# Seven-product units in parts 0 and 1 of both down projections, with tiles of their own for single blocks

## The chip, the cores and the metric

The kernel runs on one core of one Trainium2 chip. The metric is the device time of one execution in microseconds (us). Before the change the median of three runs is 2259.6 us (2258.87 to 2261.23).

## The reference, cut to what matters

A decoder of two layers on 256 tokens of width 2048: a gated linear attention layer, then a forgetting-attention layer, each followed by a channel mixer. All is fp32. The change touches only the channel mixer, whose hidden width is 5632:

```python
def conv_ffn(h, w_up, conv_w, conv_b, w_down):
    u = causal_dwconv(h @ w_up, conv_w, conv_b)
    a, val = split_cols(u, [FFN_HIDDEN, FFN_HIDDEN])
    return (jax.nn.silu(a) * val) @ w_down
...
        h = rmsnorm(x, norm_ffn[i])
        x = x + conv_ffn(h, ffn_w_up[i], conv_w[i], conv_b[i], ffn_w_down[i])
```

## The kernel before, in words

**Products.** Each fp32 matrix product is made of three float32r products: activations (the stationary side, 128x128) and weights (the moving side, 128x512) are each split into a high and a low half, and high·high, low·high and high·low are summed in PSUM. The activations lie in `A` or `B` tiles, 16 of them, one for each 128 features, with both halves.

**Weights.** They stream from HBM in units of 128x1024 (two 128-row blocks of 512 columns): a DMA on SyncE's queue into `raw` (4 buffers), a ScalarE copy to the high half `whi` (3 buffers; L207 for plain units, L308 in seven-product units) and a VectorE subtraction to the low half `wlo` (3 buffers; L216 and L310). TensorE uses a plain unit in 12 matmuls of 512 columns: 2 token blocks x 2 row blocks x 3.

**The channel mixer.** `ffn` runs three parts (`PARTS`: hidden blocks 0-16, 16-32, 32-44). Each part has the up projections of its blocks (8, 8 and 6 panels; `proj_tm`, lines L228, L229, L232) and then the down projection of those blocks onto the four 512-column panels of `x` (`add_out`). What an up panel leaves goes by VectorE transposes and a DRAM turn to feature order, then through `taken` (convolution L995 to L997, SiLU L999, product L1000, split to halves L463, L464); these steps are due 8 and 9 weight units after the panel, so those of a part's last panels run during its down projection.

**Seven-product units.** A plain pair of units (two 512-column panels, two row blocks) is a 2x2 by 2x2 block product over token blocks, row blocks and panels: 8 products, 24 matmuls. `proj_seven` does chosen units with seven products, 21 matmuls, by the Strassen-Winograd scheme. The sums of activations are made in `summed` (tiles `forms`). The sums of weights `t13` and `t24` are made on VectorE from two raw units (L333 to L336). Four pairs of halves are made: v0 (raw, 1024 wide), v1 (one raw block, 512 wide, in a full 1024-wide buffer), v2 (`t13`) and v3 (`t24`). Four of the products go to PSUM tiles of their own (m1 `ps_t`, m5 and m7 `ps_s`, m6 `ps_o`); after the last such unit `more` adds them into `x` with eight operations (L951 to L958). The four `acc` tiles, all that PSUM holds of them, are added into `x` by `evac` (L939) at the end of the call; the next call's first matmul needs the first of them free.

**Where they are used before.** `SEVEN` names the units of each part: 3 and 5, 3 and 5, 2 and 4. Layer 0 uses them in all four panels of parts 0 and 1 (two calls of `proj_seven` each) and in the first two panels of part 2, ten pairs in all. Layer 1 gets no `forms` tiles, since it holds the pool `store` (final gain `gf`, output `y`, and extra `whi`/`wlo` buffers `spare` for the last panel) from its start, so it has none: its first two panels run in `proj_two`, the others in `proj_tm`.

**What sets the order.** The code gives priorities (a unit's load and split are moved ahead by 300 places, a seven-product unit's sums by 340), and a scheduler writes each engine's instructions into one fixed order from them. Each engine then works its own list in order; an instruction that waits holds what is behind it.

Of the kernel before, what the change touches and what calls it, by code (L numbers as in the profile page):

```python
# [36 lines left out]
NVER = 96  # L37
NUNIT = 1024
AHEAD = 300
SEVEN = ((3, 5), (3, 5), (2, 4))  # L40

SPREAD = [128 * q + 32 * k + i for k in range(4) for i in range(32) for q in range(4)]

# [93 lines left out]
def _trunk(ctx: ExitStack, tc: tile.TileContext, xt, xtok, memt, wp, wgu, gns, gfin, cnv, par, msk, out):  # L137
# [131 lines left out]
    def proj_seven(keys, src, forms, evacs, pool, more):  # L269
# [33 lines left out]
        def token(kc, b):  # L303
            return [src[kc - base][:, i, b * P : (b + 1) * P] for i in range(2)]

        def halves(raw, w, name="w"):
            hi = wpool.tile([P, NUNIT], F32R, name="whi", tag="whi", bufs=3)
            casts.append(S.activation(hi[:, :w], raw, AF.Copy))  # L308
            lo = wpool.tile([P, NUNIT], F32R, name="wlo", tag="wlo", bufs=3)
            V.tensor_tensor(lo[:, :w], raw, hi[:, :w].bitcast(F32), ALU.subtract)  # L310
            return hi, lo

        def load(unit):
# [5 lines left out]
        for u in range(count):  # L319
            k0, k1 = units[0][u][1]  # L320
            if u not in forms:
                for i in range(2):
                    hi, lo = split_unit(units[i][u])
                    emit([form(acc[i][b], token(kc, b), hi, lo, c) for b in range(2) for c, kc in enumerate((k0, k1))])
                    if u == count - 1:
                        for b in range(2):
                            evacs[i](b, acc[i][b])
                continue
            s = forms[u]
            with tc.high_priority(offset=AHEAD + 40):  # L330
                r0, r1 = (load(units[i][u]) for i in range(2))
                t13, t24 = (pool.tile([P, 2, 512], F32, name=n, tag=n) for n in ("t13", "t24"))
                V.tensor_tensor(t13[:, 0, :], r1[:, :512], r0[:, :512], ALU.subtract)  # L333
# [12 lines left out]
            with tc.high_priority(offset=AHEAD):  # L346
                v3 = halves(t24.rearrange("p c n -> p (c n)"), NUNIT)
            passed()
            emit([form(m6, s(1), *v3, 0), form(acc[0][1], token(k1, 1), *v3, 1)])
            if u == max(forms):  # L350
                more(m1, m5, m6, m7, pool)

    def turned(pool, bank, width, col):

# [578 lines left out]
            add_out(("wo", 1), mix, then, late=2)  # L933


    def add_out(key, src, then=None, spare=None, late=1, forms=None, pool=None):
        def evac(f):
            def out(b, a):
                V.tensor_tensor(x[f][:, b, :], x[f][:, b, :], a, ALU.add)  # L939
                if then is not None:  # L940
                    then(f, b)

            return out

        def seven(f):
            x0, x1 = x[f], x[f + 1]

            def more(m1, m5, m6, m7, pool):
                u = pool.tile([P, 512], F32, name="u", tag="us", bufs=2)
                w = pool.tile([P, 512], F32, name="w", tag="us", bufs=2)  # L950
                V.tensor_tensor(x0[:, 0, :], x0[:, 0, :], m1, ALU.add)  # L951
                S.activation(u, m1, AF.Copy)
                V.tensor_tensor(u, u, m6, ALU.add)
# [3 lines left out]
                V.tensor_tensor(x1[:, 1, :], x1[:, 1, :], w, ALU.add)  # L957
                V.tensor_tensor(x1, x1, m5.unsqueeze(1).to_broadcast([P, 2, 512]), ALU.add)  # L958

            proj_seven([(*key, g) for g in (f, f + 1)], src, forms, [evac(f), evac(f + 1)], pool, more)  # L960

        if forms:
            seven(0)
        else:
            proj_two([(*key, f) for f in range(2)], src, [evac(f) for f in range(2)], late)
        if forms and then is None:
            seven(2)
            return
        for f in range(2, 4):
            proj_tm((*key, f), src, evac(f), spare if f == 3 else None)  # L970

    def ffn(l, nx, h, m, then, spare=None):
        with tc.tile_pool(name=f"ffn{l}", bufs=1) as fp:
# [12 lines left out]

            def taken(j, base, u, i):
# [14 lines left out]
                if (j - base) // 2 in forms[base]:  # L1002
                    held.append(cv[1])
                    if i:
                        summed(forms[base][(j - base) // 2])

            def summed(form):
                h0, h1 = (natural(h) for h in held)
                held.clear()
                f = fp.tile([P, 4, P], F32, name="sf", tag="sf")  # L1010
# [7 lines left out]
            def panel(j, base, slack=0):  # L1018
# [14 lines left out]

                return evac

            for p, (lo, hi) in enumerate(PARTS):
# [6 lines left out]
                end = p == len(PARTS) - 1  # L1043
                add_out(("down", l, p), m, then if end else None, spare if end else None,
                        forms={u: form(t) for u, t in forms[lo].items()}, pool=fp)

    def preparing(name, dst):
        n = StreamNorm()
# [28 lines left out]


    fin = StreamNorm()
    with tc.tile_pool(name="store", bufs=1) as op:  # L1080
# [29 lines left out]
        ffn(1, n, bufA, bufB, then, op)  # L1110


def _constants():
# [82 lines left out]
```

## Time and profile before

| what | value |
| --- | --- |
| median of three runs | 2259.6 us |
| the profiled execution | 2260.52 us |
| its span, first to last instruction | 2258.7 us |
| mean granted TensorE clock | 0.999 |
| layer 0, down projection of part 0 (L290) | 645.1 to 732.1 us |
| the same of part 1 | 906.3 to 993.4 us |
| layer 0, part 2, first two panels (L290) | 1124.1 to 1159.9 us |
| layer 1, down projection of part 0 (plain) | 1704.9 to 1791.9 us |
| the same of part 1 | 1966.0 to 2053.1 us |

The profile is of one execution. All times in it are in us from its first instruction. In a timeline a row has start, duration, engine, source line, operation, output and inputs with shape, a count if the row merges several instructions of one kind that follow each other, and in brackets how long the engine had been idle before and what ended it. "PE" is TensorE's matmul, "DVE" VectorE, "ACT" ScalarE, "SPq" a DMA issued by SyncE. A matmul's duration (about 0.39 us here) is longer than the distance from one to the next, since they overlap; in a row that merges n of them, the distance is (duration - 0.39) / (n - 1).

### The profile page before, as it was taken

Reading aid. Unit: us, or ns where it says so; the run is one execution under the profiler, and the core shown is the slowest. Engines: PE = TensorE matmul, PEld = TensorE weight load, DVE = VectorE, ACT = ScalarE, POOL = GpSimd, SP = SyncE. Lnnn points to the kernel's source line nnn. Section 1 sums busy time; section 2 is a strip of 40 time slices with the busy share of each in tenths; the row PEclk is TensorE's granted clock in tenths of the full one; section 3 lists DMA queues with packets and bytes.
Section 4 is the critical chain, followed back from the end, with each engine's and each line's share of the span. In section 5 each row is a group of like instructions: output and inputs, shape, how many; then the busy total and the mean of one; then the engine's idle time right before and its main releaser. Section 6 shows DMA issues by size and latency. Waiting matters only on the chain.

```text
span 2258.7 us, 29424 instructions
## 1 busy us (share of the span) xinstructions
PE 2238.1 (99%) x10306; PEld 1866.9 (83%) x10306; DVE 1595.0 (71%) x2442; ACT 1298.8 (58%) x1881; POOL 2.9 (0%) x15
## 2 busy tenths in 40 slices
PE   9999999999999999999999999999999999999998
PEld 7888887888878888788878998888888888888886
DVE  7568987667778677876786656766776467754766
ACT  7555666556664566545665655555665355544654
POOL 0000000000000000000000000000000000000000
PEclk9999999999999999999999999999999999999999
DMA  8876666677876778658778886677877677766784
GB/s 318 279 234 190 207 202 215 194 244 243 252 214 205 236 239 242 207 200 247 238 234 249 259 270 202 179 246 235 251 242 226 195 236 243 242 202 209 239 244 149
DMA packets 303772, 516.97 MB, mean 229 GB/s; under 512 B 178556, under 2 KB 187272, under 8 KB 303496
## 3 DMA queue, kind: packets, MB, share of 16 engines
q1 hardware_dynamic: 124296, 427.24, 59.1%
q10 hardware_dynamic: 179328, 87.85, 13.8%
q8 instruction: 81, 1.33, 0.2%
q14 instruction: 67, 0.55, 0.1%
HBM read 470.44 MB, written 44.58 MB: 228 GB/s over the span
## 4 chain that ended last, share of the span: by engine, by line
PE 94%; DMA 2%; DVE 2%; ACT 1%; issue 1%; ACTq 0%; SPq 0%; DVEq 0%
PE acc L228 28%; PE acc L229 28%; PE acc L232 28%; PE acc L290 7%; DMA xturned<-square 1%; PE ps_s L290 1%; DVE wlo L216 0%; PE ps_s L768 0%; DMA raw<-wp 0%; DMA cb<-cdram 0%; PE ps_s L570 0%; PE ps_t L563 0%; ACT whi L207 0%; PE ps_o L581 0%; DMA back<-turned 0%
## 5 line engine op out<-in xcount | busy, mean ns | idle before, releaser
L216 DVE TENSOR_TENSOR wlo<-raw,whi 128x1024 fp32r<-128x1024 f32 (+4 forms) x789 | 942.9, 1199 | 550.0 <-ACT whi L207 520.6
L207 ACT ACTIVATE whi<-raw 128x1024 fp32r<-128x1024 f32 (+4 forms) x789 | 820.6, 1042 | 792.7 <-PE acc L229 575.5
L228 PE MATMUL acc<-whi,B 128*128 128x512 f32 (+3 forms) x1792 | 686.1, 384 | 1.0 <-ACT whi L207 0.8
L229 PE MATMUL acc<-whi,B 128*128 128x512 f32 (+3 forms) x1792 | 684.5, 383 | 0.0
L232 PE MATMUL acc<-wlo,B 128*128 128x512 f32 (+3 forms) x1792 | 470.0, 382 | 0.0
L228 PE MATMUL acc<-whi,A 128*128 128x512 f32 x1136 | 443.7, 392 | 1.5 <-ACT A L463 1.0
L229 PE MATMUL acc<-whi,A 128*128 128x512 f32 x1136 | 441.4, 390 | 0.0
L228 PEld LDWEIGHTS acc<-whi,B 128*128 128x128 f32 x1792 | 336.3, 188 | 62.8 <-ACT whi L207 1.6
L229 PEld LDWEIGHTS acc<-whi,B 128*128 128x128 f32 x1792 | 336.0, 188 | 59.5
L232 PEld LDWEIGHTS acc<-wlo,B 128*128 128x128 f32 x1792 | 333.5, 188 | 59.8
L232 PE MATMUL acc<-wlo,A 128*128 128x512 f32 x1136 | 305.6, 390 | 0.2 <-DVE wlo L216 0.2
L228 PEld LDWEIGHTS acc<-whi,A 128*128 128x128 f32 x1136 | 213.1, 188 | 48.3 <-ACT whi L207 2.0
L232 PEld LDWEIGHTS acc<-wlo,A 128*128 128x128 f32 x1136 | 213.0, 188 | 44.7 <-DVE wlo L216 0.7
L229 PEld LDWEIGHTS acc<-whi,A 128*128 128x128 f32 x1136 | 213.3, 188 | 44.2 <-DVE A L467 0.4
L290 PE MATMUL acc<-whi,A 128*128 128x512 f32 x488 | 127.5, 391 | 3.4 <-DVE A L464 1.4
L995 ACT ACTIVATE cv<-u,cw 128x256 f32<-128x256 f32 x176 | 97.2, 589 | 25.8 <-DMA u<-turned 25.6
L290 PEld LDWEIGHTS acc<-whi,A 128*128 128x128 f32 x488 | 91.1, 188 | 25.1 <-DVE A L464 1.8
L996 DVE SCALAR_TENSOR_TENSOR cv<-u,cw,cv 128x256 f32<-128x256 f32 x176 | 78.4, 478 | 18.0 <-ACT cv L995 18.0
L383 DVE STREAM_TRANSPOSE square<-scaled 128x512 f32<-128x512 f32 x122 | 79.9, 690 | 0.0
L997 DVE SCALAR_TENSOR_TENSOR cv<-u,cw,cv 128x256 f32<-128x256 f32 x176 | 77.2, 476 | 0.0
L290 PE MATMUL acc<-wlo,A 128*128 128x512 f32 x244 | 68.3, 390 | 0.0
L1025 ACT ACTIVATE scaled<-acc,ny 128x512 f32<-128x512 f32 x88 | 54.9, 674 | 0.0
(221 smaller groups left out, 1234.8 us busy)
## 6 DMA issues: line engine op xcount, KB each, us to landing
raw<-wp SPq DMA_DIRECT2D x743, 512.0 KB, 4.2
turned<-square ACTq DMA_DIRECT2D x61, 512.0 KB, 4.2
u<-turned ACTq DMA_DIRECT2D x176, 128.0 KB, 5.1
raw<-wp SPq DMA_DIRECT2D x32, 384.0 KB, 3.5
raw<-wp SPq DMA_DIRECT2D x24, 388.0 KB, 4.5
back<-xturned ACTq DMA_DIRECT2D x64, 128.0 KB, 5.2
xturned<-square ACTq DMA_DIRECT2D x12, 512.0 KB, 4.8
back<-turned ACTq DMA_DIRECT2D x32, 128.0 KB, 4.4
```

Of the source, the lines that this page charges most:

```text
L207: casts.append(S.activation(hi[:, s], raw[:, s], AF.Copy))
L216: V.tensor_tensor(lo[:, s], raw[:, s], hi[:, s].bitcast(F32), ALU.subtract)
L228: TE.matmul(acc[:, :n], xh, hi[:, s], start=first and j == 0, stop=False)
L229: TE.matmul(acc[:, :n], xl, hi[:, s], start=False, stop=False)
L232: TE.matmul(a, xh, ls, start=False, stop=stop)
L290: TE.matmul(a, x, w, start=k not in begun, stop=calls[k] == 0)
L383: V.transpose(self.square[:, :, :, b], src.rearrange("p (c t) -> p c t", t=32))
L995: S.activation(r, v[:, 2:], AF.Identity, bias=w[3], scale=w[2])
L996: V.scalar_tensor_tensor(r, v[:, 1 : T + 1], w[1], r, ALU.mult, ALU.add)
L997: V.scalar_tensor_tensor(r, v[:, :T], w[0], r, ALU.mult, ALU.add)
L1025: S.activation(e, a, AF.Copy, scale=nx.col()[:, b : b + 1])
```

## The change

- `SEVEN` is now (3, 5) and holds for parts 0 and 1 of both layers; the last parts have none. That is 8 pairs in each layer, 16 in all.
- In a seven-product unit the single block v1 no longer takes a full `whi` and `wlo` buffer: it has tiles `vhi` and `vlo` of its own, 512 wide.
- The two sums of `more` get tiles of their own (`s16`, `s167`).
- All these tiles, with `forms`, `t13` and `t24`, lie in a pool `sums` that is closed before the last part. In layer 1 the pool `store` is opened only then (`ending`), so the load of `gf` moves from ahead of layer 1's channel mixer to the end of its part 1.

```diff
-SEVEN = ((3, 5), (3, 5), (2, 4))
+SEVEN = (3, 5)
...
-        def halves(raw, w, name="w"):
-            hi = wpool.tile([P, NUNIT], F32R, name="whi", tag="whi", bufs=3)
-            casts.append(S.activation(hi[:, :w], raw, AF.Copy))
-            lo = wpool.tile([P, NUNIT], F32R, name="wlo", tag="wlo", bufs=3)
-            V.tensor_tensor(lo[:, :w], raw, hi[:, :w].bitcast(F32), ALU.subtract)
+        def halves(raw, w):
+            if w == NUNIT:
+                hi, lo = (wpool.tile([P, w], F32R, name=n, tag=n, bufs=3) for n in ("whi", "wlo"))
+            else:
+                hi, lo = (pool.tile([P, w], F32R, name=n, tag=n) for n in ("vhi", "vlo"))
+            casts.append(S.activation(hi, raw, AF.Copy))
+            V.tensor_tensor(lo, raw, hi.bitcast(F32), ALU.subtract)
...
+    def add_seven(key, src, forms, pool):
+        for f in (0, 2):
+            def more(m1, m5, m6, m7, x0=x[f], x1=x[f + 1]):
+                u, w = (pool.tile([P, 512], F32, name=n, tag=n) for n in ("s16", "s167"))
...
+            proj_seven([(*key, g) for g in (f, f + 1)], src, forms, [add_panel(g) for g in (f, f + 1)], pool, more)
...
-            tiles = [fp.tile([P, 2, 4, P], F32R, name=f"forms{i}") for i in range(2 if spare is None else 0)]
-            forms = {lo: dict(zip(us, tiles)) for (lo, _), us in zip(PARTS, SEVEN)}
+            forms = {u: sp.tile([P, 2, 4, P], F32R, name=f"forms{u}") for u in SEVEN}
...
+                if p == len(PARTS) - 1:
+                    sums.close()
+                    if ending is not None:
+                        then, spare = ending(ends)
...
+                if p < len(PARTS) - 1:
+                    add_seven(("down", l, p), m, {u: form(t) for u, t in forms.items()}, sp)
+                    continue
+                add_out(("down", l, p), m, then, spare)
```

Ahead of layer 0's first down projection the engines' lists are the same. In the down projections they differ as follows (the lines of the changed file lie one to five off: L333 to L336 are L335 to L338, L310 is L312, L996 is L991, L951 to L958 are L955 to L962, L939 is L940).

VectorE's list at the first seven-product pair of layer 0, part 0, before; `t_6199` and `t_6200` are its `t13` and `t24`, `t_6306` is the second pair's `t13`:

```order
L336 TENSOR_TENSOR t_6200<-raw,t_6200 128x512
L310 TENSOR_TENSOR wlo<-raw,whi 128x512
L310 TENSOR_TENSOR wlo<-t_6199,whi 128x1024
L333 TENSOR_TENSOR t_6306<-raw 128x512
L334 TENSOR_TENSOR t_6306<-raw 128x512
L310 TENSOR_TENSOR wlo<-t_6200,whi 128x1024
L996 SCALAR_TENSOR_TENSOR cv_6236<-u_4577,cw,cv_6236 128x256
```

And after the change (`t_6202`, `t_6203` and `t_6309` in the same roles):

```order
L312 TENSOR_TENSOR vlo<-raw,vhi 128x512
L337 TENSOR_TENSOR t_6203<-raw,t_6202 128x512
L312 TENSOR_TENSOR wlo<-raw,whi 128x1024
L338 TENSOR_TENSOR t_6203<-raw,t_6203 128x512
L312 TENSOR_TENSOR wlo<-t_6202,whi 128x1024
L312 TENSOR_TENSOR wlo<-t_6203,whi 128x1024
L991 SCALAR_TENSOR_TENSOR cv_6239<-u_4580,cw,cv_6239 128x256
L335 TENSOR_TENSOR t_6309<-raw 128x512
L336 TENSOR_TENSOR t_6309<-raw 128x512
```

The low half of v3 (from `t24`) and one step of the convolution now stand ahead of the second pair's first sums, behind which they stood before.

VectorE's list at the end of the same call, before, from the last additions of `more` to the first release of `acc`:

```order
L955 TENSOR_TENSOR w<-u,ps_s 128x512
L216 TENSOR_TENSOR wlo<-raw,whi 128x1024
L956 TENSOR_TENSOR x_80<-x_80,w 128x512
L957 TENSOR_TENSOR x_81<-x_81,w 128x512
L939 TENSOR_TENSOR x_80<-x_80,acc 128x512
L216 TENSOR_TENSOR wlo<-raw,whi 128x1024
L939 TENSOR_TENSOR x_80<-x_80,acc 128x512
L958 TENSOR_TENSOR x_81<-x_81,ps_s 128x1024
```

And after:

```order
L959 TENSOR_TENSOR s_6353<-s_6352,ps_s 128x512
L216 TENSOR_TENSOR wlo<-raw,whi 128x1024
L960 TENSOR_TENSOR x_80<-x_80,s_6353 128x512
L961 TENSOR_TENSOR x_81<-x_81,s_6353 128x512
L216 TENSOR_TENSOR wlo<-raw,whi 128x1024
L962 TENSOR_TENSOR x_81<-x_81,ps_s 128x1024
L940 TENSOR_TENSOR x_80<-x_80,acc 128x512
```

The 1024-wide addition into `x` and one more weight split now stand ahead of the first release of `acc`. The number of weight splits (L216) from the second pair's sums to that release is seven in both lists. The same lists stand in part 1 of layer 0 and in parts 0 and 1 of layer 1.

SyncE's list at the end of layer 1's part 1 after the change; L318 are the loads of seven-product units, L206 those of plain ones:

```order
L318 DMA raw<-wp 128x1024 x2
L206 DMA raw<-wp 128x1024 x2
L318 DMA raw<-wp 128x1024 x2
L206 DMA raw<-wp 128x1024 x7
L1085 DMA gf<-gfin 128x2048
L206 DMA raw<-wp 128x1024 x69
```

The load of `gf` waits there for VectorE, TensorE and GpSimd, since its tile takes the place of those of `sums`; 69 weight loads are queued behind it.

TensorE's list has 18 matmuls fewer. In layer 0's part 2 it now reads as that of layer 1's part 2 does before, up to the last panel.

More of the change, by code (lines that the diff above doesn't have):

```diff
@@ L350, in proj_seven @@
             if u == max(forms):
-                more(m1, m5, m6, m7, pool)
+                more(m1, m5, m6, m7)
     def turned(pool, bank, width, col):
@@ L933, in fox, with add_panel, out, add_out @@
             add_out(("wo", 1), mix, then, late=2)
[L936 to L950, printed above, removed]
+    def add_panel(f, then=None):
+        def out(b, a):
+            V.tensor_tensor(x[f][:, b, :], x[f][:, b, :], a, ALU.add)
+            if then is not None:
+                then(f, b)
+        return out
+    def add_out(key, src, then=None, spare=None, late=1):
+        proj_two([(*key, f) for f in range(2)], src, [add_panel(f, then) for f in range(2)], late)
+        for f in range(2, 4):
+            proj_tm((*key, f), src, add_panel(f, then), spare if f == 3 else None)
+    def add_seven(key, src, forms, pool):
+        for f in (0, 2):
+            def more(m1, m5, m6, m7, x0=x[f], x1=x[f + 1]):
+                u, w = (pool.tile([P, 512], F32, name=n, tag=n) for n in ("s16", "s167"))
                 V.tensor_tensor(x0[:, 0, :], x0[:, 0, :], m1, ALU.add)
@@ L958, in more, with ffn @@
                 V.tensor_tensor(x1, x1, m5.unsqueeze(1).to_broadcast([P, 2, 512]), ALU.add)
[L960 to L973, printed above, removed]
+            proj_seven([(*key, g) for g in (f, f + 1)], src, forms, [add_panel(g) for g in (f, f + 1)], pool, more)
+    def ffn(l, nx, h, m, then, ending=None):
+        with tc.tile_pool(name=f"ffn{l}", bufs=1) as fp, ExitStack() as ends:
+            sums = ends.enter_context(ExitStack())
+            sp = sums.enter_context(tc.tile_pool(name=f"sums{l}", bufs=1))
             cw = fp.tile([P, 4 * 88], F32, name="cw")
@@ L1001, in taken @@
                 split(m, j + i - base, cv[1])
-                if (j - base) // 2 in forms[base]:
+                if base < PARTS[-1][0] and (j - base) // 2 in forms:
                     held.append(cv[1])
                     if i:
-                        summed(forms[base][(j - base) // 2])
+                        summed(forms[(j - base) // 2])
             def summed(form):
@@ L1009, in summed @@
                 held.clear()
-                f = fp.tile([P, 4, P], F32, name="sf", tag="sf")
+                f = sp.tile([P, 4, P], F32, name="sf", tag="sf")
                 V.tensor_tensor(f[:, 0, :], h0[:, :, 1], h1[:, :, 1], ALU.add)
@@ L1079, in _trunk, with ending @@
     fin = StreamNorm()
-    with tc.tile_pool(name="store", bufs=1) as op:
+    def ending(ends):
+        op = ends.enter_context(tc.tile_pool(name="store", bufs=1))
         gf = op.tile([P, D], F32, name="gf")
@@ L1108, in then @@
                 (nc.scalar if g == 1 else nc.sync).dma_start(out[b, :, g * 512 : (g + 1) * 512], t)
-        ffn(1, n, bufA, bufB, then, op)
+        return then, op
+    ffn(1, n, bufA, bufB, None, ending)
 def _constants():
```

4 lines of the change are left out of this document (1 added, 3 removed).

## The prediction

> **What bounds the kernel now.** First the page: engines, then the granted clock.
>
> ```profile
> PE 2238.1 (99%) x10306; PEld 1866.9 (83%) x10306; DVE 1595.0 (71%) x2442; ACT 1298.8 (58%) x1881; POOL 2.9 (0%) x15
> PEclk9999999999999999999999999999999999999999
> ```
>
> TensorE (PE) works 99% of the span at full clock, so what counts is the number of matmuls and the few places where it waits. A busy PE need not be a PE at its peak, so next comes the view of busy time by stretches, for PE: layer 1's plain stretch first, then layer 1's down projection of part 0, and, for line L290 alone, layer 0's three stretches with seven-product units.
>
> ```profile
> core 0: us, PE busy (x), PEclk, DMA share, GB/s
> 1510.00:2249.00 739.00, 739.00 (x3261) 1.00 0.73 225
> 1704.90:1791.90 87.00, 87.00 (x385) 1.00 0.68 209
> ...
> 645.10:732.10 87.00, 86.16 (x372) 1.00 0.62 202
> 906.30:993.40 87.10, 86.15 (x372) 1.00 0.62 202
> 1124.10:1159.90 35.80, 32.37 (x138) 1.00 0.66 206
> ```
>
> Layer 1 pays 739.00 / 3261 = 0.2266 us for a matmul and never waits. Layer 0's part 0 does 12 matmuls less than layer 1's (372 against 384; the count 385 includes an edge) in the same 87.0 us: **seven-product units as they stand gain nothing**. At 0.2266 us, 372 matmuls are 84.3 us, so 2.7 are lost in part 0 and 2.8 in part 1; in part 2, 138 are 31.3 us of 35.8, so 4.5 are lost, against 6 matmuls (1.4 us) saved. The sum of losses is 10.0.
>
> Where are the 2.7 us? VectorE (DVE) busy by stretches of part 0's first call (to 689.2) and second call:
>
> ```profile
> 660.00:664.60 4.60, 1.23 (x1) 1.00 0.68 232
> 664.60:689.20 24.60, 24.59 (x36) 1.00 0.54 173
> 689.20:732.00 42.80, 35.25 (x41) 1.00 0.61 200
> ```
>
> It stands nearly idle for 4.6 us and is then full without a gap for 24.6, to the end of the call. The timeline of DVE, ScalarE (ACT) and PE shows why, and what PE waits for:
>
> ```profile
> 661.77 1.23 DVE L310 TENSOR_TENSOR wlo<-t,whi 128x1024 fp32r<-128x1024 f32 x1 [1.92 <-ACT whi L308]
> 664.61 0.69 DVE L333 TENSOR_TENSOR t<-raw 128x512 f32<-128x512 f32 x1 [1.62 <-DMA raw<-wp]
> 665.83 1.22 DVE L310 TENSOR_TENSOR wlo<-t,whi 128x1024 fp32r<-128x1024 f32 x1
> 666.96 0.87 DVE L996 SCALAR_TENSOR_TENSOR cv<-u,cw,cv 128x256 f32<-128x256 f32 x2
> 688.47 0.67 DVE L939 TENSOR_TENSOR x<-x,acc 128x512 f32<-128x512 f32 x1
> 690.80 1.20 DVE L958 TENSOR_TENSOR x<-x,ps_s 128x1024 f32<-128x1024 f32 x1
> ...
> 662.54 1.06 ACT L308 ACTIVATE whi<-t 128x1024 fp32r<-128x1024 f32 x1 [0.80 <-PE acc L290]
> ...
> 660.47 1.07 PE L290 MATMUL acc<-wlo,A 128*128 128x512 f32 x4
> 667.10 0.50 PE L290 MATMUL ps_o<-wlo,forms 128*128 128x512 f32 x1 [0.23 <-DVE wlo L310]
> 677.04 1.20 PE L290 MATMUL acc<-whi,A 128*128 128x512 f32 x4 [0.39 <-ACT whi L207]
> 687.19 1.98 PE L290 MATMUL acc<-wlo,A 128*128 128x512 f32 x8
> 689.29 1.16 PE L290 MATMUL acc<-whi,A 128*128 128x512 f32 x4
> ```
>
> v3's high half (662.54) waited until PE had read a buffer; its low half then stood behind L333, which waited for a load, so PE waited at 667.10. Further on PE waited at 677.04. At the end of the call, the eight matmuls from 687.19 would let the next one start at 687.19 + 8 x 0.227 = 689.0, and it starts at 689.29, just after L939 has freed `acc` at 689.14: DVE and PE end together, so a shorter PE alone would gain nothing.
>
> **The change part by part.**
>
> *Matmuls.* Ten pairs become sixteen, three matmuls less each: -18, at 0.2266 us -4.1 us. The Trainium skill ("TensorE: Matmul & The Clock Gate", section "Back-to-back issue gap") gives about 131 ns for a sustained matmul of 512 columns; by that, an estimate, the 18 would be worth 2.4 us. The row of 739 us over 3261 matmuls shows 227 ns, and the measurement decides.
>
> *Part 2 of layer 0, first two panels.* Its waits, from the view of waits in that stretch:
>
> ```profile
> PE acc L290 <- DVE A L464: 1.4, 1, 1.4
> PE ps_o L290 <- DVE wlo L310: 1.1, 1, 1.1
> PE acc L290 <- ACT A L463: 1.0, 1, 1.0
> ```
>
> They are of a seven-product pair next to the end of a short call, with the last activations late behind its vector work. With plain units PE's list is that of layer 1's part 2, which lies in the 739 us without a wait: 144 x 0.2266 = 32.6 us in place of 35.8, **-3.2 us**. Bounds: 1.0 us less, the shortest of the three waits, if layer 0's norm work, which layer 1 lacks, costs one; not more than 3.2, since PE has nothing left to save.
>
> *The order in the first call of a part.* With `vhi` and `vlo`, v0, v2 and v3 take three buffers where v0 to v3 took four, so v3 takes a buffer of the plain unit ahead, whose last matmuls are those from 660.47, done by 661.5. ACT's copy can run from then, and DVE's subtraction at about 661.8 to 663.0, in the idle stretch, ahead of L333 (which waits for its load until 664.6 as before). So the wait at 667.10 goes, and most of that at 677.04. **What is late next is the release of `acc`.** From L333 to it DVE has the same work as before, less one subtraction (1.14, the distance of 665.83 to 666.96) and one L996 (0.4, half of the pair at 666.96), plus L958 (1.13 of its 1.20), which now stands ahead: 689.14 - 664.61 = 24.5, -1.14 - 0.40 + 1.13 = 24.1 us. The release falls to 688.7, 0.45 us earlier, and that is all that the first call gains. PE will be ready before: of the 2.7 us, 0.4 are slower matmuls (below) and 0.3 each the waits at the two calls' ends, so some 1.7 lie inside the first call, and without them PE waits for the release for 1 to 1.5 us.
>
> *The order in the second call.* The rows of its end:
>
> ```profile
> 723.21 0.40 PE L290 MATMUL ps_o<-wlo,forms 128*128 128x512 f32 x1
> 732.08 0.47 PE L228 MATMUL acc<-whi,B 128*128 128x512 f32 x1
> 723.71 0.69 DVE L953 TENSOR_TENSOR u<-u,ps_o 128x512 f32<-128x512 f32 x1 [1.23 <-PE ps_o L290]
> 731.26 0.68 DVE L939 TENSOR_TENSOR x<-x,acc 128x512 f32<-128x512 f32 x1
> ```
>
> DVE waits for m6's last matmul, then needs 8.2 us to the release (731.94), and PE's next matmul starts at 732.08, 8.87 us after 723.21, where 38 matmuls need 8.6: 0.3 us of waiting. After the change 46 matmuls stand from there to the end of the call, 8 more (1.8 us), and DVE has the same nine operations to the release. So it is done 1.5 us before PE needs it, and the 0.3 goes. Bounds: 0 to 0.3.
>
> Together a part with two calls loses 2.7 - 0.45 - 0.3 = 1.95 us, **-0.75** for each of layer 0's two.
>
> *Layer 1's parts 0 and 1.* They get the same lists, so I take the same loss: 372 x 0.2266 + 1.95 = 86.25 in place of 87.0 us, **-0.75** each. The activation sums in the up projections go beside TensorE's work: layer 0's up panels pay for them already, at 71% DVE over the span, and are not among the waits. Bounds for the loss: 2.7 (nothing improves) and 0.4 (only what stays if every wait goes). The 0.4 are the matmuls with `forms`:
>
> ```profile
> 655.94 2.20 PE L290 MATMUL acc<-whi,A 128*128 128x512 f32 x9
> 663.44 1.10 PE L290 MATMUL ps_s<-whi,forms 128*128 128x512 f32 x4
> ```
>
> They follow each other by (1.10 - 0.39) / 3 = 0.237 against (2.20 - 0.39) / 8 = 0.226 us, and there are 48 in a part.
>
> *The load of `gf`.* It waits for the last use of `sums`, with weight loads behind it. The place in layer 0's part 1 that answers to it (SyncE, DVE, ACT):
>
> ```profile
> 965.26 0.89 SPq L316 DMA_DIRECT2D raw<-wp  x2
> 973.39 35.68 SPq L206 DMA_DIRECT2D raw<-wp  x16
> 989.70 0.68 DVE L957 TENSOR_TENSOR x<-x,w 128x512 f32<-128x512 f32 x1
> 992.44 1.06 ACT L207 ACTIVATE whi<-raw 128x1024 fp32r<-128x1024 f32 x1 [1.66 <-PE acc L290]
> 998.24 1.06 ACT L207 ACTIVATE whi<-raw 128x1024 fp32r<-128x1024 f32 x1 [4.74 <-PE acc L229]
> ```
>
> Seven loads come first, so the eighth would start near 973.39 + 7 x 2.36 = 989.9 and now waits for L957, done at 990.4: half a us to one and a half late, with `gf` ahead of it. The copies near 998 wait 4.7 us for buffers, not for loads, and cover this; without that cover it costs at most the 1.5. I take nothing.
>
> *Sum:* -1.5 (layer 0, parts 0 and 1) - 3.2 (part 2) - 1.5 (layer 1) = **-6.2 us**, the 18 matmuls among them. The profiled execution (2260.5, span 2258.7) would become 2254.3; it lies 0.9 above the median of the runs, so the prediction is 2259.6 - 6.2 = **2253.4 us**.
>
> **The rivals.**
>
> *The waits stay as they are* (2.7 in every part of both layers): the buffers weren't what delayed the halves, or other waits fill the place. Parts 0 and 1 give 0 in both layers, as layer 1 against layer 0 shows now, and only part 2 gains: -3.2, **2256.4 us**. For it speaks that DVE is full for 24.6 us whatever the buffers do; against it the 4.6 idle us ahead, into which the lists move work.
>
> *The waits go.* The Trainium skill ("Perfetto Trace Analysis", section "Optimization Strategy" under "Identifying Performance Opportunities") says that a gap which repeats on the engine that should be saturated can mean too little buffer space for the next tile. As a mechanism here: buffers alone held up the halves, and with tiles of their own each of four parts loses only 0.4. Then each gains 2.3: -4 x 2.3 - 3.2 = -12.4, **2247.2 us**. For it speaks the repeated row of ACT waiting for PE's reading; against it the 24.59 of 24.60.
>
> *DVE's list turns against it: slower.* v3's low half now stands ahead of L333. Should it come when it came before (done at 667.05, then 0.4 for L996), L333 starts at 667.4, and the 24.1 us put the release at 691.5, 2.4 us later than now, in the first call of all four parts: 4 x 2.4 - 3.2 = +6.4, **2266.0 us**. It decides from the point where a release comes 0.8 us later than now (3.2 / 4), that is, L333 starting after 665.8. Against it speaks that v3's buffer is free by 661.5.
>
> **How the numbers follow.** Forecast 0.52, waits stay 0.20, waits go 0.20, slower 0.08. The forecast's own range is 2251 to 2255.5. The range for 8 in 10 takes in both bounds of the loss, 2247.2 and 2256.4, with about a us on the slow side for `gf` and the norm work: 2247 to 2257.5; outside lie the slower rival and the tails. What a measurement of this kernel can tell from no change is about 0.2%, 4.5 us. Faster by more: the waits going, and 0.44 of the forecast's 0.52: 0.64. Within: the waits staying and 0.08: 0.28. Slower: 0.08.
>
> **What would show it.** In the profile after, L290 should take 86.2 to 86.4 us with 372 matmuls in each of four parts, layer 0's part 2 should show no wait, and the last wait in a part's first call should be of `acc` for `x` from L940, 1 to 1.5 us. L312 from `t24` should end before the second pair's first sums start. If PE doesn't wait at that release, DVE is not the bound and the time is nearer 2247; if L335 of the second pair starts after 665.8, it is nearer 2266. A wait for `raw` after `gf` would make the `gf` term wrong.

## The result, and the profile after

The changed kernel takes 2250.38 us, median of six runs (2248.38 to 2251.59), where the kernel before took 2258.39 in its six: a ratio of 0.9963, 95% interval 0.9950 to 0.9975, so **8.0 us less**. The prediction was 2253.4, 6.2 less than its 2259.6. The profiled execution after is 2250.39 us with a span of 2248.6; that of before was 2260.52 with 2258.7.

The engines of the page after, and then the view of busy time by stretches for L290 in the four parts that now have seven-product units (us, PE and weight-load busy time with their counts, clock, DMA share, GB/s):

```profile
PE 2232.4 (99%) x10288; PEld 1864.7 (83%) x10288; DVE 1634.8 (73%) x2509; ACT 1310.4 (58%) x1898; POOL 2.9 (0%) x15
```

```profile
643.00:728.80 85.80, 85.17 (x372) 69.55 (x371) 1.00 0.62 207
902.80:988.10 85.30, 85.09 (x372) 69.55 (x371) 1.00 0.63 208
1695.90:1783.30 87.40, 85.46 (x372) 69.40 (x371) 1.00 0.63 202
1957.30:2043.10 85.80, 85.17 (x372) 69.54 (x371) 1.00 0.65 212
```

The count of matmuls fell by 18 as worked out. Exact starts give 85.7, 85.3, 87.3 and 85.7 us for the four parts. At 0.2266 us a matmul, 372 are 84.3, so the losses are 1.4, 1.0, 3.0 and 1.4, where 1.95 each was forecast. In layer 0's last part the 288 matmuls of the down projection run from 1118.62 to 1183.89 us, 0.2266 us each. The next row is of a stretch within them that takes in nearly all of its first two panels: TensorE is never idle.

```profile
1120.00:1156.70 36.70, 36.70 (x164) 1.00 0.73 245
```

| stage | before, us | after, us | forecast | measured |
| --- | --- | --- | --- | --- |
| layer 0, part 0 | 87.0 | 85.7 | -0.75 | -1.3 |
| layer 0, part 1 | 87.1 | 85.3 | -0.75 | -1.85 |
| layer 0, part 2, two panels | 35.8 | 32.6 (144 x 0.2266) | -3.2 | -3.2 |
| layer 1, part 0 | 87.0 | 87.3 | -0.75 | +0.3 |
| layer 1, part 1 | 87.0 | 85.7 | -0.75 | -1.3 |
| sum | | | -6.2 | -7.3 |

The spans differ by 10.1 us, 2.8 more than these rows. Two waits of before lie outside the parts, in code that the change does not touch, and are absent here: 2.1 us near 382 us (the first row of the view of waits of before below) and 0.8 near 1503 us (L228 for a weight copy); against them stands one of 0.5 here (the second row of after). The first differs from one execution to the next (0.5 and 0.4 us there in the two kernels below with shared buffers), and the medians differ by 8.0, not 10.1.

The view of waits, PE alone, of before and then after (waited-for, total us, times, longest):

```profile
PE ps_s L570 <- DMA back<-turned: 2.1, 1, 2.1
PE ps_o L290 <- DVE wlo L310: 1.6, 3, 1.1
```

```profile
PE acc L290 <- DVE x L940: 3.1, 4, 1.6
PE acc L228 <- ACT whi L207: 0.7, 2, 0.5
```

The waits for v3's halves are gone and **one wait has taken their place**: `acc` at the end of the first call, once in each of the four parts (0.62, 0.21, 1.62 and 0.63 us, where 1 to 1.5 was forecast). One wait of 0.3 us for a plain unit's high half (L290 for L207) is left in layer 1's part 0. The timeline of layer 0's part 0 shows how the wait for `acc` comes about; the busy time of DVE up to it stands behind:

```profile
655.98 2.07 SPq L318 DMA_DIRECT2D raw<-wp  x2
659.74 1.23 DVE L312 TENSOR_TENSOR wlo<-t,whi 128x1024 fp32r<-128x1024 f32 x1 [0.96 <-ACT whi L311]
661.90 0.69 DVE L335 TENSOR_TENSOR t<-raw 128x512 f32<-128x512 f32 x1 [0.54 <-DMA raw<-wp]
684.25 1.23 DVE L962 TENSOR_TENSOR x<-x,ps_s 128x1024 f32<-128x1024 f32 x1
685.38 0.69 DVE L940 TENSOR_TENSOR x<-x,acc 128x512 f32<-128x512 f32 x1
683.62 1.98 PE L290 MATMUL acc<-wlo,A 128*128 128x512 f32 x8
686.22 1.17 PE L290 MATMUL acc<-whi,A 128*128 128x512 f32 x4 [0.62 <-DVE x L940]
```

```profile
661.90:686.10 24.20, 24.20 (x35) 1.00 0.54 181
```

v3's low half stands at 659.74, ahead of L335, and DVE then works without a gap from 661.90 to the release at 686.07 (685.38 + 0.69): 24.17 us, where 24.1 was forecast. PE could have gone on at 683.62 + 8 x 0.227 = 685.43 and goes on at 686.22.

### The profile page after: what moved, and what is told of

Its sections match the earlier page's. It is cut to its first block, busy times and chain, and to the rows that moved or that the text cites. A ratio compares the mean times of both kernels' runs of the same rounds, so it can differ in the third digit from the quotient of the medians.

```text
span 2248.6 us, 29488 instructions
## 1 busy us (share of the span) xinstructions
PE 2232.4 (99%) x10288; PEld 1864.7 (83%) x10288; DVE 1634.8 (73%) x2509; ACT 1310.4 (58%) x1898; POOL 2.9 (0%) x15
## 4 chain that ended last, share of the span: by engine, by line
PE 95%; DMA 2%; DVE 1%; issue 1%; ACT 0%; SPq 0%; ACTq 0%; DVEq 0%
PE acc L228 26%; PE acc L229 26%; PE acc L232 26%; PE acc L290 12%; DMA raw<-wp 1%; PE ps_s L290 1%; PE ps_o L290 0%; PE ps_t L290 0%; PE ps_s L770 0%; DVE wlo L216 0%; DMA cb<-cdram 0%; PE ps_t L565 0%; PE ps_s L572 0%; PE ps_o L583 0%; DMA values<-scaled 0%
## 5 line engine op out<-in xcount | busy, mean ns | idle before, releaser
L216 DVE TENSOR_TENSOR wlo<-raw,whi 128x1024 fp32r<-128x1024 f32 (+4 forms) x777 | 929.6, 1200 | 503.5 <-ACT whi L207 469.5
L207 ACT ACTIVATE whi<-raw 128x1024 fp32r<-128x1024 f32 (+4 forms) x777 | 808.0, 1042 | 758.0 <-PE acc L229 512.0
L228 PE MATMUL acc<-whi,B 128*128 128x512 f32 (+3 forms) x1536 | 586.2, 383 | 0.5 <-ACT whi L207 0.5
L229 PE MATMUL acc<-whi,B 128*128 128x512 f32 (+3 forms) x1536 | 584.8, 382 | 0.0
L228 PE MATMUL acc<-whi,A 128*128 128x512 f32 x1184 | 462.5, 393 | 1.3 <-ACT A L465 1.0
L229 PE MATMUL acc<-whi,A 128*128 128x512 f32 x1184 | 460.1, 390 | 0.0
L232 PE MATMUL acc<-wlo,B 128*128 128x512 f32 (+3 forms) x1536 | 401.0, 381 | 0.0
L228 PEld LDWEIGHTS acc<-whi,B 128*128 128x128 f32 x1536 | 288.2, 188 | 51.1 <-ACT whi L207 0.8
L229 PEld LDWEIGHTS acc<-whi,B 128*128 128x128 f32 x1536 | 287.9, 188 | 49.7
L232 PEld LDWEIGHTS acc<-wlo,B 128*128 128x128 f32 x1536 | 285.5, 188 | 49.9
L232 PE MATMUL acc<-wlo,A 128*128 128x512 f32 x1184 | 318.8, 390 | 0.3 <-DVE wlo L216 0.3
L228 PEld LDWEIGHTS acc<-whi,A 128*128 128x128 f32 x1184 | 222.3, 188 | 50.0 <-ACT whi L207 1.9
L232 PEld LDWEIGHTS acc<-wlo,A 128*128 128x128 f32 x1184 | 222.0, 188 | 46.6 <-DVE wlo L216 0.7
L290 PE MATMUL acc<-whi,B 128*128 128x512 f32 x416 | 108.5, 390 | 2.6 <-DVE x L940 2.2
L290 PE MATMUL acc<-whi,A 128*128 128x512 f32 x416 | 108.4, 390 | 0.8 <-DVE x L940 0.8
L290 PEld LDWEIGHTS acc<-whi,B 128*128 128x128 f32 x416 | 77.9, 188 | 20.2 <-ACT whi L207 3.8
L290 PEld LDWEIGHTS acc<-whi,A 128*128 128x128 f32 x416 | 77.9, 188 | 18.1 <-ACT whi L207 1.0
L991 DVE SCALAR_TENSOR_TENSOR cv<-u,cw,cv 128x256 f32<-128x256 f32 x176 | 78.8, 480 | 12.7 <-ACT cv L990 12.7
```

Of the source, the lines that this page charges most:

```text
L207: casts.append(S.activation(hi[:, s], raw[:, s], AF.Copy))
L216: V.tensor_tensor(lo[:, s], raw[:, s], hi[:, s].bitcast(F32), ALU.subtract)
L228: TE.matmul(acc[:, :n], xh, hi[:, s], start=first and j == 0, stop=False)
L229: TE.matmul(acc[:, :n], xl, hi[:, s], start=False, stop=False)
L232: TE.matmul(a, xh, ls, start=False, stop=stop)
L290: TE.matmul(a, x, w, start=k not in begun, stop=calls[k] == 0)
```

## The experiments

Each ratio is to the kernel before, run beside it on the same chip, with its 95% interval.

### Which part of the change does it

**Tiles of its own for the single block, nothing else** (on the kernel before):

```diff
-            hi = wpool.tile([P, NUNIT], F32R, name="whi", tag="whi", bufs=3)
...
+            if w == NUNIT:
+                hi, lo = (wpool.tile([P, w], F32R, name=n, tag=n, bufs=3) for n in ("whi", "wlo"))
+            else:
+                hi, lo = (pool.tile([P, w], F32R, name=n, tag=n) for n in ("vhi", "vlo"))
```

> The kernel before, with one edit: the single block's halves in tiles of their own; the seven-product units stay where they were (layer 0, three parts). Theory (buffers bring v3's halves ahead of the second pair's sums, and the release of the accumulators on VectorE ends the call): layer 0's parts 0 and 1 take 85.3 to 85.7 us each in place of 87.0, with a wait of 0.4 to 0.8 us for the release as the only one; part 2 keeps its waits for the last activations (it falls by at most the 1.1 us waited for v3's low half). Sum: 2.5 to 4 us faster than the kernel before. Rival (the buffers delayed nothing; what the change gained came from part 2 and from places outside): no difference, within 1 us.

2255.57 us, 0.9985 (0.9976 to 0.9994), 3.8 less. Parts 0 and 1 take 85.5 and 85.7 us, part 2 34.5. The rows of its view of waits in part 2 are the two of the last activations, which stay; that for v3's low half is gone:

```profile
PE acc L290 <- DVE A L466: 1.4, 1, 1.4
PE acc L290 <- DVE x L941: 1.0, 2, 0.6
PE acc L290 <- ACT A L465: 1.0, 1, 1.0
```

So the tiles alone change the order, and the release (the middle row) is the wait of parts 0 and 1 here too.

**Plain units in the last part, nothing else** (on the kernel before):

```diff
-SEVEN = ((3, 5), (3, 5), (2, 4))
+SEVEN = ((3, 5), (3, 5), ())
```

> The kernel before, with one edit: no seven-product units in part 2 of layer 0. Theory: its first two panels take 32.6 us in place of 35.8 without a wait, so 3.2 us faster than the kernel before. Rival (the last activations are late for plain units too, or the wait moves into the next stage): within 1 us of the kernel before.

2256.0, 0.9983 (0.9974 to 0.9992), 3.4 less for 3.2 expected. Six matmuls more and a faster kernel: no wait of part 2 is left in its view of waits; of L290 it names only two waits for a weight copy, 0.8 us together, in parts 0 and 1. These two parts, whose code is that of before, took 86.6 and 86.7 us in its profile, so they vary by some 0.4 us between executions.

**The changed kernel with seven-product units in layer 0 alone:**

```diff
-                if base < PARTS[-1][0] and (j - base) // 2 in forms:
+                if l == 0 and base < PARTS[-1][0] and (j - base) // 2 in forms:
...
-                if p < len(PARTS) - 1:
+                if l == 0 and p < len(PARTS) - 1:
...
-                add_out(("down", l, p), m, then, spare)
+                add_out(("down", l, p), m, then if p == len(PARTS) - 1 else None, spare)
```

> The changed kernel, with seven-product units in layer 0's parts 0 and 1 alone, so 24 matmuls more than the changed one. Theory (layer 1's eight pairs give back most of what their matmuls save): layer 1's two parts take 87.0 us each in place of 87.3 and 85.7, so 1 us slower than the changed kernel, 6.5 to 7.5 faster than the kernel before. Rival (the matmuls count in full): 24 x 0.2266 = 5.4 us slower than the changed kernel, 2.5 faster than before.

2252.95, 0.9974 (0.9963 to 0.9985), 6.4 less. The changed kernel's ratio puts it at 0.9963 x 2259.37 = 2251.0 in this set, so layer 1's eight pairs, 24 matmuls or 5.4 us fewer, bring some 1.9, which lies within what these intervals leave open (2.5 us each way); the table's rows of layer 1 say 1.0.

**The changed kernel with the single block in the shared buffers:**

```diff
-            if w == NUNIT:
-                hi, lo = (wpool.tile([P, w], F32R, name=n, tag=n, bufs=3) for n in ("whi", "wlo"))
...
+            hi = wpool.tile([P, NUNIT], F32R, name="whi", tag="whi", bufs=3)
```

> The changed kernel, with the single block's halves back in the shared buffers (three for all); the units are where the change puts them. Theory: the old lists come back in all four parts, each loses 2.7 us in place of 1.0 to 3.0 (mean 1.7), the waits are those for v3's low half and for a plain unit's high half, and the time is 4 us above the changed kernel, 4 below the kernel before. Rival (the tiles matter nothing): the time of the changed kernel within 1 us.

2257.91, 0.9992 (0.9983 to 1.0001): some 6.9 slower than the changed kernel, where about 4 was expected. The old lists are back, and so are the old waits (parts 87.0, 87.1, 87.2, 88.8). In layer 1's part 1 the second pair's load comes late, with v3's low half behind it:

```profile
1983.26 0.69 DVE L333 TENSOR_TENSOR t<-raw 128x512 f32<-128x512 f32 x1 [3.40 <-DMA raw<-wp]
1985.75 0.50 PE L290 MATMUL ps_o<-wlo,forms 128*128 128x512 f32 x1 [2.00 <-DVE wlo L310]
```

So DVE's list passed this late load on to TensorE. The losses of the four parts are 13.0 us against 6.8 in the changed kernel's profile: with units 3 and 5, **the tiles are worth 6 to 7 us**, most of what the change gains. In the profile some 1.6 of it are this late load, which one execution shows.

### What the release costs

**The changed kernel again**, for the set that follows:

> The changed kernel again, on the chip of the next three, to see how far its parts vary from one execution to the next. Theory: layer 0's two parts at 85.3 to 85.7 us again, layer 1's at 85.5 to 87.3, the waits at the ends of the first calls for the release of the accumulators; time 8 us below the kernel before. Rival (layer 1's part 0 is slower in itself, 87.3 each time): the same time, and 87.3 again.

2251.28, 0.9968 (0.9956 to 0.9981). Its parts take 85.7, 85.8, 86.6 and 86.0, with part 2 as in the changed kernel's first profile: -1.3 -1.3 -3.2 -0.4 -1.0 = -7.2 us, and its median is 7.3 below. The waits are the same:

```profile
PE acc L290 <- DVE x L940: 3.9, 4, 1.6
```

**The additions of `more` behind the release:** they are called after the panels' own additions.

```diff
+                if u == count - 1:
+                    more(m1, m5, m6, m7)
                 continue
...
-            if u == max(forms):
-                more(m1, m5, m6, m7)
```

> The changed kernel, with the additions of the four separate products put behind the release of the accumulators. Theory (VectorE's list sets the end of a part's first call): the release comes 4.7 us earlier in VectorE's work, no call waits for it, and the waits of 0.4 to 1.8 us with what follows them, 4.0 us in the four parts, are gone: 3 to 4 us faster than the changed kernel, 84.7 to 85.0 us a part. Rival (loads or weight halves are late at the same places, so another wait takes over): within 1 us of the changed kernel.

2247.15, 0.9949 (0.9935 to 0.9962), 4.1 less than the changed kernel beside it. All four parts take 84.8 us. DVE and PE at the same place, and L290's part 0:

```profile
683.15 1.28 DVE L940 TENSOR_TENSOR x<-x,acc 128x512 f32<-128x512 f32 x2
685.48 0.68 DVE L955 TENSOR_TENSOR x<-x,ps_t 128x512 f32<-128x512 f32 x1
684.92 1.07 PE L290 MATMUL acc<-wlo,A 128*128 128x512 f32 x4
685.83 1.07 PE L290 MATMUL acc<-whi,A 128*128 128x512 f32 x4
```

```profile
643.40:728.30 84.90, 84.90 (x372) 69.62 (x371) 1.00 0.63 210
```

The order of a few additions on an engine that is busy 73% of the span is worth 4 us. What is left above 84.3 is the slower matmuls with `forms`: 0.5, forecast 0.4.

**Units 2 and 4 in place of 3 and 5:**

```diff
-SEVEN = (3, 5)
+SEVEN = (2, 4)
```

> The changed kernel, with units 2 and 4 in place of 3 and 5, so that three plain pairs follow the last seven-product pair of a call. Theory (VectorE's list from the second pair's sums to the release, 24.1 us, must fit beside TensorE's work): the sums come 5.4 us earlier, two more weight splits (2.3 us) lie in the list, so the release is 3 us earlier and the wait for it is gone: 3 to 4 us faster than the changed kernel. Rival (the convolution of the part's last panels then falls on the second pair and its matmuls wait for weight halves): same or slower than the changed kernel.

2245.81, 0.9943 (0.9931 to 0.9956): 5.5 less than the changed kernel beside it, where 3 to 4 was expected, 12.8 less than before, and the lowest median of this set. All four parts take 84.8 us, as with the additions behind the release; the 1.3 us between the two medians are not clear of noise. The last pair, and with it `more`, comes one unit of each panel earlier (24 matmuls, 5.4 us), so its additions are done before the end of the call, and DVE now waits for PE at the release, not PE for DVE:

```profile
679.59 1.22 DVE L962 TENSOR_TENSOR x<-x,ps_s 128x1024 f32<-128x1024 f32 x1
684.30 0.69 DVE L940 TENSOR_TENSOR x<-x,acc 128x512 f32<-128x512 f32 x1 [0.98 <-PE acc L290]
```

```profile
643.00:727.90 84.90, 84.84 (x372) 69.65 (x372) 1.00 0.64 211
```

### How far it goes: more pairs, fewer matmuls

With the waits gone, each pair more should be worth three matmuls, 0.68 us. Three kernels saved 12 matmuls (2.7 us) more, with `more` behind the release. To make room in the buffers, `s16`, `s167` and the scratch of `forms` share a tile.

**Unit 1 as a third pair in the second call of each part** (beside 3 and 5):

```diff
+            forms = {u: sp.tile([P, 2, 4, P], F32R, name=f"forms{u}") for u in (1, *SEVEN)}
...
+            proj_seven(..., {u: s for u, s in forms.items() if f or u > 1}, ...)
```

> As the kernel with the release first, with a third seven-product unit (unit 1) in the second call of each part, so 12 matmuls less than the changed kernel (the sums share two tiles). Theory: VectorE had 7.5 us free in a second call; the additions that now run over into it take 4.7 and the third pair 4.1, so it is full, and of the 2.7 us of matmuls about half comes through: 1 to 2 us faster than the kernel with the release first. Rival (VectorE is no bound in a second call): 2.7 us faster than that kernel. If VectorE falls behind at the end: 1 us slower than it.

2248.66, 0.9960 (0.9947 to 0.9972): 1.5 more than without the third pair, where 1 to 2 less was expected. `more` of the first call now runs into the second, and there v3's halves stand behind it. Its waits, and the timeline of that place (its profiled execution was 2253.43 us, 4.8 above its median, so the sizes may be larger than usual):

```profile
PE ps_o L290 <- ACT whi L311: 5.5, 4, 1.9
```

```profile
694.69 1.06 ACT L311 ACTIVATE whi<-t 128x1024 fp32r<-128x1024 f32 x1 [4.41 <-DVE t L340]
695.80 0.50 PE L290 MATMUL ps_o<-whi,forms 128*128 128x512 f32 x1 [1.64 <-ACT whi L311]
```

**Unit 6 as the third pair in the second call** (beside 2 and 4; the same edit with `(6, *SEVEN)` and `if f or u < 6`):

> Units 2 and 4, the release of the accumulators ahead of the separate products' additions, and a third seven-product unit (unit 6) in the second call of each part, 12 matmuls less than with 2 and 4 alone. Theory (what sets the price of a pair is whether VectorE's list fits between it and the next release): in the second call VectorE has 7 us free, the third pair takes 4.1, the additions run over into the next up projections where it has room; but only one plain pair, 5.4 us, stands behind unit 6, and the release needs what is ahead of it in the list. I expect 2.7 us less for the matmuls and 0 to 1 us of waiting at the end of each part: 2247 to 2243 us, nearer 2244. Rival (a release so soon after a pair is late, as with units 3 and 5): 2246 us or more, with a wait at the start of the next up projections.

2246.11, 0.9939 (0.9926 to 0.9953): within the range expected, and no gain over units 2 and 4 alone (0.9943). The wait that was feared at the start of the next up projection is not there; in its place TensorE waits in the first calls, for plain high halves and for v2's low half. Layer 1's part 0 in its timeline, DVE and PE:

```profile
1711.87 0.69 DVE L337 TENSOR_TENSOR t<-raw 128x512 f32<-128x512 f32 x1 [3.23 <-DMA raw<-wp]
1722.73 0.73 PE L290 MATMUL ps_s<-wlo,forms 128*128 128x512 f32 x2 [0.29 <-DVE wlo L312]
1723.88 0.50 PE L290 MATMUL acc<-whi,B 128*128 128x512 f32 x1 [0.41 <-ACT whi L207]
```

Its parts take 84.6, 85.3, 86.3 and 84.3 us, a loss of 1.0, 1.6, 2.7 and 0.7; together that is 1.4 more than with units 2 and 4 alone. So in this execution, which lies 1.4 us above the kernel's median, all of the 2.7 us of matmuls and 1.4 more went back into waits.

**Unit 0 as a third pair in the first call** (beside 2 and 4; `(0, *SEVEN)` and `if not f or u`):

> As the last, with the third unit (unit 0) in the first call of each part instead. Theory: its sums are made during the last up panel, where VectorE has room, so the first call's list is no longer at the place where it is full: 2.7 us less than with units 2 and 4, 2243 us, with no wait in a part. Rival (the load of a pair needs two buffers at once and its sums are late behind the up projections' work): a wait at the start of a part's first call, 2245 us or more.

2257.26, 0.9991 (0.9982 to 1.0000), 14 more than expected. Its waits in the whole program, then its timeline in layer 0's part 0:

```profile
PE ps_o L290 <- ACT whi L311: 8.9, 8, 1.4
```

```profile
658.32 1.06 ACT L311 ACTIVATE whi<-t 128x1024 fp32r<-128x1024 f32 x1 [4.37 <-DVE t L340]
659.42 0.50 PE L290 MATMUL ps_o<-whi,forms 128*128 128x512 f32 x1 [1.01 <-ACT whi L311]
```

With three pairs in a row two units apart, while the late activations of the up projection also go through DVE, the sums of weights come out too late, and v3's high half behind them. Three pairs were more than DVE had room for in this first call; other places for a third were not tried.

### Tiles or place?

The runs so far had left both: shared buffers lose with units 3 and 5, and units 2 and 4 win with tiles. **Units 2 and 4 with the single block in the shared buffers** (the edits of the kernels with shared buffers and with units 2 and 4 together):

> Units 2 and 4 with the single block's halves in the shared buffers. Theory (two causes apart: with shared buffers v3's halves are late inside the call, with units 3 and 5 the release is late at its end): the release is in time, but the waits for v3's low half and a plain unit's high half stay, some 1.2 us in each first call: 4 to 6 us slower than units 2 and 4 with tiles of their own. Rival (VectorE's list alone was the cause, the tiles only moved it): within 1 us of units 2 and 4 with tiles.

2249.03, 0.9950 (0.9938 to 0.9963). The expectation was wrong: the four parts take 84.9 us each, 0.4 us more in all than with tiles of its own. So the tiles are not needed with these units. The order on DVE is the old one, v3's low half behind the next unit's first sums, but the load ahead of it is waited for less, and TensorE's list has more in front of the matmul that needs it. Here, and then before (units 3 and 5):

```profile
657.09 0.69 DVE L333 TENSOR_TENSOR t<-raw 128x512 f32<-128x512 f32 x1 [0.83 <-DMA raw<-wp]
658.30 1.22 DVE L310 TENSOR_TENSOR wlo<-t,whi 128x1024 fp32r<-128x1024 f32 x1
658.82 3.13 PE L290 MATMUL acc<-whi,A 128*128 128x512 f32 x13
661.79 0.40 PE L290 MATMUL ps_o<-wlo,forms 128*128 128x512 f32 x1
```

```profile
665.54 1.32 PE L290 MATMUL acc<-whi,A 128*128 128x512 f32 x5
667.10 0.50 PE L290 MATMUL ps_o<-wlo,forms 128*128 128x512 f32 x1 [0.23 <-DVE wlo L310]
```

With units 2 and 4 the low half is done at 659.52, and the thirteen matmuls in front (2.9 us) keep TensorE at work until 661.79. With units 3 and 5 it was done at 667.05, and the five in front (1.1 us) ended at 666.68. Five matmuls would have lasted until 658.82 + 5 x 0.227 = 659.95 in the first case, so in this call the load came early enough by itself (DVE waits 0.83 us for it, against 1.62); the thirteen add room. The median is about 3 us above that of units 2 and 4 with tiles, but the two were run in different sets: by the ratios it is some 1.6 us, and the intervals overlap. The parts account for 0.4 us; whether the rest is real was not settled.

## Why the prediction was right, and where its sizes were off

*Matmuls and part 2.* Right: 18 fewer, and -3.2 us in part 2, which the second experiment measured alone as -3.4.

*The order in the first call.* The mechanism was right: the tiles let v3's low half go ahead of L335 (the first and fourth experiments), the inside waits went, and **the release of `acc` was late next**, on a list of 24.17 us where 24.1 was worked out. That DVE's list up to the release is the bound was shown by the kernel with the additions behind the release: the same matmuls and additions, no wait. In all eight first calls of the two profiles of the changed kernel this list takes 24.15 to 24.18 us from L335 to the release, so the release moves with L335 alone.

The size was off: "waits for its load until 664.6 as before" failed. L335 needs both of the pair's loads, and each waits for a free `raw`. With shared buffers the second waits for v1's split, and that split cannot start before TensorE has given back a buffer: this load goes out 14.8 us after the call's start in both parts of before and in three of the four of the kernel with shared buffers. With `vhi` and `vlo` v1 is split earlier, and the load follows DVE's work on the first pair: in seven of the eight calls it goes out 5.5 us after the first pair's second load has landed, and 5.8 in the eighth. The rows are of the loads before, and of v1's split in the kernel with shared buffers, where the wait is longer than before; the loads of after are above.

```profile
659.14 1.06 SPq L316 DMA_DIRECT2D raw<-wp  x2
```

```profile
658.21 0.69 DVE L310 TENSOR_TENSOR wlo<-raw,whi 128x512 fp32r<-128x512 f32 x1 [0.44 <-PE acc L290]
```

In layer 0's part 0 the first load goes out 13.0 us after the call's start, where it was 14.1, and the second at 14.7, where it was 14.8. The second takes 4.07 us to land, where it took 4.61. That it lands sooner because the first is further ahead would fit, but no run shows it. So L335 starts 18.9 us into the call instead of 19.5, and the release comes 1.0 us earlier than before (43.09 after the call's start, where it was 44.08), not 0.45. That is the term of the sum that was mis-sized: the list's length was right, and its start was taken as fixed. In the eight calls it lies between 18.5 and 20.5 us, where it was 19.55 and 19.62 before.

*The order in the second call.* Right: no wait at its end, 0.3 us gained. Layer 0's part 0 thus gains 1.0 + 0.3 = 1.3 where 0.45 + 0.3 was forecast.

*Layer 1.* "The same lists, so the same loss" holds in the second of its two parts (a loss of 1.4) and not in the first (3.0), mainly because the same list starts from a load that can land late:

```profile
1709.34 2.07 SPq L318 DMA_DIRECT2D raw<-wp  x2
1716.40 0.69 DVE L335 TENSOR_TENSOR t<-raw 128x512 f32<-128x512 f32 x1 [2.13 <-DMA raw<-wp]
1739.88 0.68 DVE L940 TENSOR_TENSOR x<-x,acc 128x512 f32<-128x512 f32 x1
1740.70 1.17 PE L290 MATMUL acc<-whi,B 128*128 128x512 f32 x4 [1.62 <-DVE x L940]
```

The loads went out 13.4 us into the call and the sums began 7.1 us later (5.9 in layer 0's part 0); the list then takes its 24.2 us to 1740.56, and PE waits 1.62. Of the 1.6 us that this part loses beyond the second, 1.0 is this longer wait, and 0.6 goes with the wait for a plain unit's high half that was named above. The second profile of the changed kernel has a wait of the same size for the release there (1.6 is its longest) and not the other, and loses 2.3. Why these two loads take longer was not tried.

*The load of `gf`.* Right, nothing: it goes out at 2037.51 us, the view of waits names no wait of TensorE from 2030 to 2070, and in the 20 us behind the part's end TensorE works without a gap.

```profile
2037.51 0.33 SPq L1085 DMA_DIRECT2D gf<-gfin  x1
```

```profile
2043.10:2063.10 20.00, 20.00 (x90) 1.00 0.67 239
```

*The rivals.* "The waits stay" fell with the first and fourth experiments: without the tiles they stay, with them they go. "The waits go" was not this kernel but the next one: it needs the release out of the way, and then the parts take what that rival said (84.8, a loss of 0.5 for 0.4) and the time is 2247.15 and 2245.81 for its 2247.2. Of the Trainium skill's rule ("Perfetto Trace Analysis", section "Optimization Strategy") that a repeating gap can mean too little buffer space, this case shows both sides: with units 3 and 5 the tiles took away the gap that repeated and left another, and with units 2 and 4 neither gap is there, tiles or not. "DVE's list turns against it" did not occur: L335 starts at 661.90, far from 665.8.

*The sum.* None of the four parts took the 86.2 to 86.4 us that were forecast: three were 0.5 to 1.0 us better than 86.25 and one 1.05 worse, so that the sum came closer than its terms, which is in part luck. It is -7.3 us in the parts, against -6.2; the median's remaining 0.7 is within what executions vary by. The forecast came out right to 3.0 us in the time, 1.8 of them in the change itself, the rest the change of the median of before between its two sets of runs.

## What to carry to other kernels

When a wait is taken away, work out which engine's list ends next, from the point where it last stood idle to the release that the busy engine needs: here 24.1 us of additions and splits set the time. Work out also what the list starts from: here it was a load, and its landing moved the release by up to 2 us from call to call. Putting the additions behind the release, or making them ready 5.4 us earlier, took off another 4 and 5.5 us beyond the change's 8. Where work stands in another engine's list can also do what extra buffers do: with the units one place earlier the shared buffers cost 0.4 us in the parts. Fewer matmuls are worth their time only as long as the engine that prepares them has room; with a third pair in a call, waits took all of it back, or more.

## What the runs showed of the hardware that was not expected

In the run with unit 1 as third pair, TensorE's granted clock fell for one stretch of about 3.4 us after a wait in layer 1's part 0. L290 by stretches:

```profile
1748.00:1751.00 3.00, 1.08 (x5) 0.57 (x5) 1.00 0.61 209
1751.00:1755.00 4.00, 4.00 (x12) 3.13 (x11) 0.57 0.27 89
1751.20:1754.50 3.30, 3.30 (x9) 2.61 (x8) 0.50 0.18 72
1755.00:1759.00 4.00, 4.00 (x19) 3.28 (x18) 1.00 0.32 122
```

The wait itself was 1.92 us; behind it 12 matmuls took the time of 18. Waits as long left the clock at 1.00: the 2.1 us of before near 382, and 2.00 us in the run with shared buffers, whose four us behind the wait hold 19 matmuls. The Trainium skill ("TensorE: Matmul & The Clock Gate", section "What's actually happening") says that the clock halves after an idle window of some 3.4 us and returns after a busy one of the same length. The length of the slow stretch agrees; that a wait of 1.92 us was enough does not, and why this one and not the others is open. This wait thus cost its own length and 1.6 us more (eight matmuls at 0.427 us in place of 0.227).

Each wait of TensorE also cost a little beyond itself: the matmul after it is followed late, as in the row at 686.22 (1.17 us for four, where four take 0.39 + 3 x 0.227 = 1.07).
